# Four moves in one encoder kernel: a split behind a bank's copy, weights in token tiles, stores issued by ScalarE, an earlier load

## The chip, the core and the metric

The kernel runs on one core of a Trainium2 chip. The time is the device time of one execution in microseconds (us). The engines are named as in the profile: PE (TensorE, matmuls; PEld its weight loads), DVE (VectorE), ACT (ScalarE), POOL (GpSimd) and SP (SyncE, which issues nearly all transfers).

## The reference, cut to what matters

One encoder layer with two groups of heads over the same normalised input, for two sequences with the same weights: the prompt (512 tokens) and the sample (1024 tokens).

```python
def mixer_layer(x, norm_g, w_in, w_dw, b_dw, ln_g, ln_b, w_pw, sink, w_out):
    h = rms_norm(x, norm_g)
    z = h @ w_in                      # 2048 -> 3*1024 + 2*1024 + 2*256
    c_val, c_glu, c_gate, q, k, v, a_gate = split(z)
    q, k = apply_rope(q), apply_rope(k)
    conv_out = conformer_conv(c_val, c_glu, w_dw, b_dw, ln_g, ln_b, w_pw) * silu(c_gate)
    attn_out = banded_sink_attention(q, k, v, sink) * silu(a_gate)   # window 128, sinks
    return x + concatenate([conv_out, attn_out]) @ w_out
# encoder: the layer, then rms_norm, for x_prompt and for x_sample; all in float32
```

## The kernel before, in words

**Matmuls in three passes.** Float32 operands are split into a high part and a low rest (`parts`, L499 and L500: ScalarE copies the high part, VectorE subtracts it to get the low one), and each product of 128x128 weights with 128x512 tokens is three matmuls: high with high, high with low, low with high.

**Units.** The sample's projections run as units of seven products in place of eight (a Strassen scheme). A `Unit` covers 8 weight tiles of 128x128 in each of two column blocks. It has two raw loads (`load0`, `load1`) and four weight operands made from them (`make0` to `make3`). The products run in the order P1, P2, P6, P5, P7, P3, P4, 12 matmuls each; P1 and P2 use the first operand, P6 and P5 the second, P7 and P3 the third, P4 the fourth. P1 writes bank a, P2 bank b, P6 adds onto bank a, P5 writes bank c, P7 adds onto bank a, P3 onto c, P4 onto a. When a product is done, `tap` takes its bank up: for all but P2 and P3 ScalarE copies the bank (L226), and VectorE adds. P6 can start only when P1's bank a has been copied. The third operand is a subtraction on VectorE (L142), the split's high part on ScalarE (L499) and the low part on VectorE (L500). Most items of the program are one unit ("lone"); a few are two side by side. `Onto` is a unit that adds its products onto tiles on VectorE (L293) without a copy by ScalarE.

**Jobs.** The prompt's projections and others are plain jobs (`Job`, 48 matmuls each, L652) with two weight loads. Some read the low part back from memory, where the units had stored it, and ScalarE then makes the high part alone (L407).

**Order and rings.** `run` goes through the items; around the matmuls it calls `w_prep`, which makes operands ahead of their use (`look` of them) and issues the next loads, and `tick`, which lets three lanes of other work (convolution, attention, sums) move on at given rates. The instructions are put into each engine's queue by priority: `URGENT` work is placed early, `issue_after` keeps an instruction behind another. An engine runs its queue in order, so an instruction that waits holds all behind it. Tiles come from rings: 3 raw weight buffers, 3 split operands, 4 each of "a", "g", "u" and "p", 7 of "f". A load into a ring's tile waits until the former tile there is no longer read.

**The places.** The sample's last gates: `silu_of` makes the gate's Silu on ScalarE and stores it (`store` issues on SP, L493). The last unit before the prompt's jobs (`end`) also splits the prompt's tokens (`follow`, `load_two`, from xr_d, mostly in "a" tiles). `prompt.jobs()` follow: `pj[0]` is the prompt's first job, with the attention of the sample beside it. Late in the jobs `attention_sums` runs (L1266, L1267), and after it the prompt's attention group by group: `group` loads keys and values (k_d, v_d) into "a" tiles and the query (q_d) into a "u" tile.

Of the kernel before, what the change touches and what calls it, by code (L numbers as in the profile page):

```python
# [7 lines left out]
F32 = mybir.dt.float32  # L8
# [85 lines left out]
class Unit:  # L94
# [34 lines left out]
    late = False  # L129
    look = NHL  # L130
# [31 lines left out]
    def make2(self):  # L162
        self.sub(self.r2[:, 0], self.r2[:, 1], self.r2[:, 0])
        if self.sums:
            self.e.store(self.sums["P7"], self.r2[:, 0])
        t = self.e.hl_tile()
# [19 lines left out]
    def product(self, step, late):  # L186
# [11 lines left out]
        for j in range(HALF):  # L198
# [21 lines left out]
    def tap(self, name):  # L220
# [3 lines left out]
        if name not in ("P2", "P3"):  # L224
            t = e.E()
            nc.scalar.activation(t, bank, AF.Copy)  # L226
        if name == "P1":
# [147 lines left out]
class Job:  # L375


    behind = False
# [7 lines left out]
    def preps(self, e):  # L386
        def one(k):
# [3 lines left out]
            def load():  # L391
                st["raw"] = e.raw_tile()
# [27 lines left out]
class Encoder:  # L420
# [203 lines left out]
    def run(self, items):  # L624
# [3 lines left out]
        for n, item in enumerate(items):  # L628
# [3 lines left out]
            if isinstance(item[0], Unit):  # L632
                for u in item:
                    u.open()
# [93 lines left out]
class Sequence:  # L728


    def __init__(self, e, s):
# [3 lines left out]
        self.hT = {}  # L735
        nc = e.nc
# [358 lines left out]
    def group(self, g):  # L1095
# [7 lines left out]
        held = []  # L1103
        for src in (self.k_d[g], self.v_d[g]):
            held.append(e.A([self.T], F32))
            nc.sync.dma_start(held[-1], src)
        self.load_query(g, 0)
# [7 lines left out]
    def load_query(self, g, b):  # L1115
        if b < self.B:
            self.q = self.e.U([GROUP, P])
# [66 lines left out]
    def units(self):  # L1184
# [16 lines left out]
        for i in range(0, NC, 2):  # L1201
            done = each(self.silu_of(self.gate_d[i]), self.silu_of(self.gate_d[i + 1]))
# [29 lines left out]
class Mix:  # L1232
# [590 lines left out]
def encoder(ctx, tc, a):  # L1823
# [161 lines left out]
    pj[0].behind = True  # L1985
# [13 lines left out]
    def prepare():  # L1999
# [4 lines left out]
        e.attn.add(mix.attention_sums())  # L2004
# [120 lines left out]
```

## Time and profile before

| | us |
|---|---|
| three runs | 2091.29, 2093.96, 2093.98 (median 2093.96) |
| the profiled execution | 2092.61 |
| its span, first to last instruction | 2090.8 |
| PE, DVE, ACT, POOL busy | 2063.2, 1753.9, 1046.4, 77.4 |

The mean clock granted to TensorE was 0.997 of full speed. In the rows of the trace stand the start and the duration in us, the engine and its line, what is written and read with the shape, how many such instructions stand together (x12), and in brackets how long the engine stood idle before and what ended that wait. A matmul's end is modelled, and matmuls overlap; so starts are the safer numbers.

### The profile page before, as it was taken

How to read it: one execution, taken by the hardware profiler on the slowest of the kernel's cores; microseconds unless marked ns; L12 is line 12 of the kernel's file. 1: busy time of each engine (PE TensorE's matmuls, PEld its weight loads, DVE VectorE, ACT ScalarE, POOL GpSimd, SP SyncE). 2: the span in 40 equal slices, each digit the busy share in tenths (PEclk: the TensorE clock that was granted, in tenths of full speed). 3: DMA queues.
4: the chain of work that ended last, by engine and by line, in shares of the span. 5: the costliest groups of instructions: out<-in, count | busy, mean ns of one | idle time of the engine just before them, and what ended most of it. 6: DMA issues, size and time to landing. Idle time of an engine off the chain costs nothing.

```text
span 2090.8 us, 27085 instructions
## 1 busy us (share of the span) xinstructions
PE 2063.2 (99%) x9259; PEld 1695.2 (81%) x9259; DVE 1753.9 (84%) x2877; ACT 1046.4 (50%) x1711; POOL 77.4 (4%) x92
## 2 busy tenths in 40 slices
PE   9999999999999999999999999999999999999998
PEld 8878888888887778778888888887888878888886
DVE  8758899998899999999556877776899978898887
ACT  7476435333464344544456777336454343454454
POOL 0001110000001112100000000000000000000000
PEclk9999999999999999999999999999999999999999
DMA  8988887865577676945455565996789889678897
GB/s 279 320 294 244 204 214 234 292 201 170 181 240 194 169 170 179 273 153 161 162 170 185 168 193 166 324 334 222 242 291 300 282 291 318 211 246 297 290 332 269
DMA packets 251194, 494.54 MB, mean 237 GB/s; under 512 B 23600, under 2 KB 84400, under 8 KB 251056
## 3 DMA queue, kind: packets, MB, share of 16 engines
q1 hardware_dynamic: 238384, 469.75, 67.0%
q0 software_dynamic: 12672, 23.07, 6.6%
q8 instruction: 72, 1.18, 0.2%
q14 instruction: 66, 0.54, 0.1%
HBM read 331.77 MB, written 160.96 MB: 236 GB/s over the span
## 4 chain that ended last, share of the span: by engine, by line
PE 51%; DVE 8%; DMA 4%; issue 3%; ACT 1%; SPq 0%; POOL 0%; ACTq 0%; DVEq 0%; POOLq 0%
PE a L652 13%; PE c L652 7%; PE b L652 6%; PE a L200 6%; PE c L200 3%; PE pv L1166 2%; PE s L1137 2%; PE a L1800 2%; PE s L1800 2%; DVE hl L500 1%; PE b L200 1%; PE pt L1171 1%; PE pv L1800 1%; PE pt L1800 1%; DVE f L1020 1%
## 5 line engine op out<-in xcount | busy, mean ns | idle before, releaser
L200 PE MATMUL a<-t,hl 128*128 128x512 f32 x2640 | 634.0, 391 | 7.8 <-ACT g L226 3.6
L200 PEld LDWEIGHTS a<-t,hl 128*128 128x128 f32 x2640 | 492.8, 188 | 117.2 <-ACT u L226 6.0
L499 ACT ACTIVATE hl<-raw 128x1024 fp32r<-128x1024 f32 (+3 forms) x334 | 297.2, 890 | 394.1 <-PE c L200 85.6
L500 DVE TENSOR_TENSOR hl<-raw,hl 128x1024 fp32r<-128x1024 f32 (+3 forms) x334 | 338.5, 1014 | 134.0 <-ACT hl L499 132.8
L652 PE MATMUL a<-t,hl 128*128 128x512 f32 x1344 | 329.3, 395 | 2.0 <-ACT hl L499 1.4
L200 PE MATMUL c<-t,hl 128*128 128x512 f32 x1320 | 319.9, 390 | 0.6 <-DVE u L293 0.6
L652 PEld LDWEIGHTS a<-t,hl 128*128 128x128 f32 x1344 | 249.4, 189 | 53.0 <-ACT hl L499 1.9
L200 PEld LDWEIGHTS c<-t,hl 128*128 128x128 f32 x1320 | 247.2, 188 | 52.6 <-DVE u L293 1.5
L1020 DVE SCALAR_TENSOR_TENSOR f<-f,c_w_dw,f 128x512 f32<-128x512 f32 x248 | 175.3, 748 | 0.3
L652 PE MATMUL c<-t,hl 128*128 128x512 f32 x672 | 165.4, 394 | 0.0
L652 PE MATMUL b<-t,hl 128*128 128x512 f32 x672 | 163.5, 392 | 0.2 <-DVE hl L500 0.2
L983 DVE SCALAR_TENSOR_TENSOR f<-f,c_w_dw,f 128x512 f32<-128x512 f32 x232 | 163.3, 745 | 0.2 <-ACT f L978 0.2
L200 PE MATMUL b<-t,hl 128*128 128x512 f32 x660 | 160.1, 389 | 0.0
L652 PEld LDWEIGHTS b<-t,hl 128*128 128x128 f32 x672 | 124.9, 188 | 25.3 <-DVE hl L500 0.7
L652 PEld LDWEIGHTS c<-t,hl 128*128 128x128 f32 x672 | 125.3, 189 | 24.7
L200 PEld LDWEIGHTS b<-t,hl 128*128 128x128 f32 x660 | 123.7, 188 | 25.5
L1012 DVE SCALAR_TENSOR_TENSOR f<-f,w_both,f 128x512 f32<-128x512 f32 x120 | 89.9, 749 | 1.8
L407 ACT ACTIVATE hl<-raw 128x1024 fp32r<-128x1024 f32 x44 | 46.5, 1057 | 61.6 <-PE a L652 22.6
L226 ACT ACTIVATE u<-a 128x512 f32<-128x512 f32 x82 | 48.6, 592 | 56.1 <-PE a L200 50.8
L226 ACT ACTIVATE g<-a 128x512 f32<-128x512 f32 x78 | 46.2, 593 | 56.7 <-PE a L200 54.4
L499 ACT ACTIVATE a<-pt 128x512 fp32r<-128x512 f32 x64 | 38.0, 594 | 68.3 <-PE pt L1171 68.2
L1151 ACT ACTIVATE p<-p,tiny 128x384 f32<-128x384 f32 (+1 forms) x96 | 54.5, 570 | 33.0 <-DVE tiny L1148 22.5
(332 smaller groups left out, 2637.7 us busy)
## 6 DMA issues: line engine op xcount, KB each, us to landing
raw<-w_in SPq DMA_DIRECT2D x171, 512.0 KB, 5.0
raw<-w_out SPq DMA_DIRECT2D x31, 512.0 KB, 5.0
raw<-w_pw SPq DMA_DIRECT2D x24, 512.0 KB, 4.2
wsum_P<-raw SPq DMA_DIRECT2D x47, 256.0 KB, 3.5
raw<-wsum_P SPq DMA_DIRECT2D x18, 512.0 KB, 4.6
f<-x_s SPq DMA_DIRECT2D x16, 512.0 KB, 7.2
g<-wsum_P SPq DMA_DIRECT2D x28, 256.0 KB, 4.4
a<-sum_S SPq DMA_DIRECT2D x24, 256.0 KB, 5.8
```

The lines of the kernel that those rows point to most:

```text
L200: nc.tensor.matmul(acc, hl[:, l, o, j, :], toks[j][:, r], start=name in FRESH and j == 0 and q == 0, stop=name in LAST and j == HALF - 1 a ...
L226: nc.scalar.activation(t, bank, AF.Copy)
L407: e.nc.scalar.activation(t[:, 0], raw, AF.Copy)
L499: nc.scalar.activation(hi, x, AF.Copy)
L500: nc.vector.tensor_tensor(lo, x, hi.bitcast(F32), ALU.subtract)
L652: nc.tensor.matmul(job.acc[0], hl[:, l, kk // HALF, kk % HALF, :], r, start=i == 0 and p == 0, stop=i == nk - 1 and p == 2,)
L983: nc.vector.scalar_tensor_tensor(t, h[:, j : j + T], w(j), t, ALU.mult, ALU.add)
L1012: nc.vector.scalar_tensor_tensor(m0, odd[:, j : j + H], both(j), m0, ALU.mult, ALU.add)
L1020: nc.vector.scalar_tensor_tensor(out, d[:, j : j + H], w(2 * j + k), out if j else m0, ALU.mult, ALU.add)
L1137: nc.tensor.matmul(ps[:, 0:n], qs[:, x, h], k[y][:, keys], start=p == 0, stop=p == 2)
L1151: nc.scalar.activation(p[:, 0:n], p[:, 0:n], AF.Exp, bias=nm[:, h : h + 1], accum_out=l[:, h : h + 1])
L1800: nc.tensor.matmul(acc[t], self.toks[name, m][:, x, i, t * P : (t + 1) * P], parts[i][l].rearrange("p a b -> p (a b)"), start=fresh and fi ...
```

## The change

Four edits.

1. The third operand's subtraction is separated (`less2`). In a lone unit VectorE does it during P1 (`lessen`), where before the whole third operand was prepared. The split follows in step 1, during P2, and is kept behind the last copy of a bank by ScalarE (`issue_after(self.copied)`). For `Onto` units there is no such copy and only the step changes.
2. The prompt's first job loads both its weight tiles into "a" tiles and not into the raw ring (`early`).
3. The sample's gates 4 to 7 (of 8) are stored by ScalarE's own queue: eight transfers.
4. The prompt's first keys, values and query are loaded into "p" tiles just before the last step of `attention_sums` (`fetch_first`), not after it into "a" and "u" tiles.

```diff
+    def less2(self):
+        self.sub(self.r2[:, 0], self.r2[:, 1], self.r2[:, 0])
+        if self.sums:
+            self.e.store(self.sums["P7"], self.r2[:, 0])
+        self.lessened = True
+
     def make2(self):
-        self.sub(self.r2[:, 0], self.r2[:, 1], self.r2[:, 0])
-        if self.sums:
-            self.e.store(self.sums["P7"], self.r2[:, 0])
+        if not self.lessened:
+            self.less2()
         t = self.e.hl_tile()
-        self.e.parts(t[:, 0], t[:, 1], self.r2)
+        with self.e.tc.issue_after(self.copied) if self.copied else ExitStack():
+            self.e.parts(t[:, 0], t[:, 1], self.r2)
...
-                e.w_prep(i + self.look)
+                if step or not self.alone:
+                    e.w_prep(i + self.look)
+                else:
+                    e.lessen(self)
...
             nc.scalar.activation(t, bank, AF.Copy)
+            self.copied = nc.cur_bb.bb.instructions[-1]
...
-                st["raw"] = e.raw_tile()
+                st["raw"] = e.A([2, HALF, P], F32) if self.early else e.raw_tile()
...
+    def lessen(self, unit):
+        if self.ready == unit.at[2]:
+            with ExitStack() if self.calm else self.tc.high_priority(URGENT):
+                unit.less2()
...
-    def silu_of(self, dst):
+    def silu_of(self, dst, own=False):
+        queue = self.e.nc.scalar if own else self.e.nc.sync
...
-            self.e.store(dst[:, t * W : t * W + W], z)
+            queue.dma_start(dst[:, t * W : t * W + W], z)
...
-            done = each(self.silu_of(self.gate_d[i]), self.silu_of(self.gate_d[i + 1]))
+            done = each(*(self.silu_of(self.gate_d[j], i >= 4) for j in (i, i + 1)))
...
+    def fetch_first(self):
+        self.held[0] = self.fetch(0, lambda: self.e.PT("p", NP, [W]))
+        self.load_query(0, 0, self.e.PT("p", NP, [GROUP, P]))
...
-    def attention_sums(self):
+    def attention_sums(self, then):
...
         for j in range(HALF):
+            if j == HALF - 1:
+                then()
...
-    pj[0].behind = True
+    pj[0].behind = pj[0].early = True
...
-        e.attn.add(mix.attention_sums())
+        e.attn.add(mix.attention_sums(prompt.fetch_first))
```

Three places show what moves. Lines below 126 keep their numbers or shift by one; L226, L493 and L499 of before are L236, L504 and L510 of the changed kernel. ScalarE in the last unit but one before the prompt's jobs; `hl_908` of before and `hl_910` of the changed kernel are the third operand, `g_911` and `g_909` P1's copy. Before:

```order
L226 ACTIVATE u_907_7216<-a_889_7061 128x512
L499 ACTIVATE hl_904_7195<-p_903_7191 128x512
L499 ACTIVATE hl_908_7220<-raw_892_7072 128x1024
L226 ACTIVATE g_911_7239<-a_906_7212 128x512
L499 ACTIVATE hl_912_7257<-raw_888_7049 128x512
```

and in the changed kernel:

```order
L236 ACTIVATE u_907_7216<-a_889_7061 128x512
L510 ACTIVATE hl_904_7195<-p_903_7191 128x512
L236 ACTIVATE g_909_7234<-a_906_7212 128x512
L510 ACTIVATE hl_910_7236<-raw_894_7088 128x1024
L510 ACTIVATE hl_912_7257<-raw_888_7049 128x512
```

The third operand's split and the copy have changed places.

SP's queue where the prompt's first job is fed; `raw_945` and `a_945` are the second half of job 0's weights, `raw_959` and `raw_964` the two halves of job 1's, `xr_d` the prompt's tokens, `k_d0`, `v_d0` and `q_d0` the sample's keys, values and query. Before:

```order
L393 DMA raw_945_7447<-w_in 128x1024
L399 DMA hl_946_7449<-low_kv0_0_361 128x1024
L1963 DMA a_937_7407<-xr_d1_7_193 128x1024
L493 DMA gate_d0_5_93<-g_918_7318 128x512
L493 DMA gate_d0_5_93<-u_914_7277 128x512
L1106 DMA a_970_7589<-k_d0_0_104 128x1024
L1106 DMA a_971_7591<-v_d0_0_106 128x1024
L393 DMA raw_959_7515<-w_in 128x1024
L493 DMA gate_d0_4_92<-u_931_7380 128x512
L1118 DMA u_972_7593<-q_d0_0_108 128x4x128
L493 DMA gate_d0_6_94<-g_939_7413 128x512
L393 DMA raw_964_7581<-w_in 128x1024
```

In the changed kernel, where `raw_959` stands further ahead, in the row that was job 0's first half's:

```order
L1995 DMA a_925_7366<-xr_d1_3_189 128x1024
L410 DMA hl_946_7449<-low_kv0_0_361 128x1024
L404 DMA raw_964_7581<-w_in 128x1024
L1995 DMA a_936_7406<-xr_d1_6_192 128x1024
L1995 DMA a_937_7408<-xr_d1_7_193 128x1024
L404 DMA a_945_7447<-w_in 128x1024
L404 DMA raw_976_7633<-w_in 128x1024
L1148 DMA u_972_7593<-q_d0_0_108 128x4x128
L412 DMA hl_965_7583<-low_kv0_1_362 128x512
L1138 DMA a_970_7589<-k_d0_0_104 128x1024
L1138 DMA a_971_7591<-v_d0_0_106 128x1024
```

The gates' stores are gone, the weights of job 1 come ahead of job 0's second half, the query ahead of keys and values, and a token tile (`a_925`) is loaded here that was loaded further ahead before.

ScalarE at the same place in the changed kernel; `gate_d` rows are the stores it now issues:

```order
L510 ACTIVATE hl_961_7552<-a_921_7347 128x1024
L982 ACTIVATE g_939_7414<-g_939_7414 128x512
L982 ACTIVATE u_931_7380<-u_931_7380 128x512
L983 DMA gate_d0_6_94<-g_939_7414 128x512
L983 DMA gate_d0_4_92<-u_931_7380 128x512
L418 ACTIVATE hl_946_7449<-a_945_7447 128x1024
L236 ACTIVATE g_973_7596<-a_930_7376 128x512
L418 ACTIVATE hl_965_7583<-raw_964_7581 128x1024
L510 ACTIVATE a_984_7698<-u_972_7593 128x512
L514 ACTIVATE t1_955_7501<-a_937_7408,c_norm_g_278 128x512
L514 ACTIVATE t1_956_7504<-a_937_7408,c_norm_g_278 128x512
L510 ACTIVATE hl_975_7630<-raw_959_7515 128x1024
```

The query's split (`a_984`) stands ahead of the prompt's last tokens (`t1_955`, `t1_956`) and of job 1's first operand (`hl_975`); two stores stand between the operands of job 0.

More of the change, by code (lines that the diff above doesn't have):

```diff
@@ L129 @@
     late = False
+    alone = lessened = copied = False
     look = NHL
@@ L160, in make1 @@
         return t
-    def make2(self):
+    def less2(self):
         self.sub(self.r2[:, 0], self.r2[:, 1], self.r2[:, 0])
@@ L165, in make2 @@
             self.e.store(self.sums["P7"], self.r2[:, 0])
+        self.lessened = True
+    def make2(self):
+        if not self.lessened:
+            self.less2()
         t = self.e.hl_tile()
-        self.e.parts(t[:, 0], t[:, 1], self.r2)
+        with self.e.tc.issue_after(self.copied) if self.copied else ExitStack():
+            self.e.parts(t[:, 0], t[:, 1], self.r2)
         self.r2 = None
@@ L375 @@
 class Job:
-    behind = False
+    behind = early = False
     def __init__(self, w, ks, n, rhs, evac, before=None, low=None):
@@ L633, in run @@
                 for u in item:
+                    u.alone = len(item) == 1
                     u.open()
@@ L735, in __init__ @@
         self.hT = {}
+        self.held = {}
         nc = e.nc
@@ L1102, in group @@
             k, v = [(t[:, 0], t[:, 1]) for t in kv]
[L1103 to L1107, printed above, removed]
+        held = self.held.pop(g, None)
+        if not held:
+            held = self.fetch(g, lambda: e.A([self.T], F32))
+            self.load_query(g, 0)
         yield e.attn.rate * LEAD * (1 + (self.s and g == 0))
```

10 lines of the change are left out of this document (8 added, 2 removed).

## The prediction

> **What bounds the kernel now.** I read the profile's page first, then the waits of TensorE, then the timeline of TensorE around each wait, and beside it that of the engine that ended it.
>
> The page's line of busy times:
>
> ```profile
> PE 2063.2 (99%) x9259; PEld 1695.2 (81%) x9259; DVE 1753.9 (84%) x2877; ACT 1046.4 (50%) x1711; POOL 77.4 (4%) x92
> L200 PE MATMUL b<-t,hl 128*128 128x512 f32 x660 | 160.1, 389 | 0.0
> ```
>
> TensorE (PE) is busy for 99% of the span of 2090.8 us and the change takes no matmul away, so all that can be gained are the places where it stands still or runs slowly. The second line counts the units: 12 matmuls fall on bank b in each, 660 / 12 = 55 units of seven products. The view of TensorE's waits names what it stood still for (total, times, longest):
>
> ```profile
> PE a L200 <- ACT g L226: 3.6, 4, 1.4
> PE s L1137 <- DVE tiny L1140: 2.5, 1, 2.5
> PE a L200 <- ACT u L226: 2.4, 5, 0.8
> PE s L1137 <- ACT a L499: 1.6, 1, 1.6
> PE a L652 <- ACT hl L499: 1.4, 1, 1.4
> PE s L724 <- DVE u L719: 1.2, 1, 1.2
> PE a L200 <- DVE u L293: 1.0, 2, 0.8
> ```
>
> Together 13.7 us, so this change deals in microseconds and not in per cents. 0.2% of the time (4.2 us) is about what a measurement of this kernel can tell from no change.
>
> **Part 1, the third operand's split.** TensorE, ScalarE (ACT) and VectorE (DVE) in one lone unit, by the timeline (start, duration; idle before in brackets):
>
> ```profile
> 669.59 2.91 PE L200 MATMUL b<-t,hl 128*128 128x512 f32 x12
> 673.80 3.03 PE L200 MATMUL a<-t,hl 128*128 128x512 f32 x12 [1.30 <-ACT g L226]
> 676.67 2.88 PE L200 MATMUL c<-t,hl 128*128 128x512 f32 x12
> 679.39 0.85 PE L200 MATMUL a<-t,hl 128*128 128x512 f32 x3
> 671.44 0.68 DVE L142 TENSOR_TENSOR raw<-raw 128x512 f32<-128x512 f32 x1
> 672.21 1.06 ACT L499 ACTIVATE hl<-raw 128x1024 fp32r<-128x1024 f32 x1 [4.68 <-issue]
> 673.17 0.58 ACT L226 ACTIVATE g<-a 128x512 f32<-128x512 f32 x1
> ```
>
> P2 (bank b) starts at 669.59, so P1 on bank a was issued by then, and its copy (L226) could have run some 2 us before P6 wants the bank. It ran only at 673.17, because the split of the third operand (L499) stands ahead of it and waits for VectorE's subtraction, which ended at 672.12. A product takes 679.39 − 676.67 = 2.72 us; from P2's start to P6's it took 4.21. The stall so costs 1.49 us, 0.2 more than the idle time shown.
>
> In the changed program the copy stands ahead of the split. The copy then needs only the bank, and 2.72 us of P2 cover its 0.58 us and an activation of 1.06 us that may still be running: the stall goes to nothing. The split comes 0.6 us later on ScalarE, and its operand is wanted at P7 only, four products or 10.9 us after the unit's start, so that is covered too. The waits from 600 to 850 us:
>
> ```profile
> PE a L200 <- ACT g L226: 2.3, 3, 1.3
> PE a L200 <- ACT u L226: 1.1, 3, 0.4
> ```
>
> Six stalls, 3.4 us idle, and with 0.17 us of restart each **4.4 us**; all six are of P2-to-P6 kind. The same edit takes the split out of three other places:
>
> ```profile
> 150.97 0.50 PE L724 MATMUL s<-u,ones_r 128*128 128x512 f32 x1 [1.20 <-DVE u L719]
> 149.31 1.22 DVE L500 TENSOR_TENSOR hl<-raw,hl 128x1024 fp32r<-128x1024 f32 x1
> 166.09 4.19 PE L200 MATMUL a<-t,hl 128*128 128x512 f32 x17 [0.82 <-ACT u L226]
> 163.44 1.28 ACT L499 ACTIVATE t<-p 128x512 fp32r<-128x512 f32 x2 [2.03 <-DMA p<-sum_S]
> 1809.61 2.99 PE L200 MATMUL a<-t,hl 128*128 128x512 f32 x12 [0.79 <-DVE u L293]
> 1807.03 1.23 DVE L500 TENSOR_TENSOR hl<-raw,hl 128x1024 fp32r<-128x1024 f32 x1
> 1808.77 0.69 DVE L293 TENSOR_TENSOR u<-a,u 128x512 f32<-128x512 f32 x1
> ```
>
> At 150.97 TensorE waits for four small VectorE operations between which the split's low half (1.22 us) was put; it now stands behind them: 1.20 + 0.17, say **1.4 us**. At 166.09 the copy stood behind splits that waited 2.03 us for a load; it now stands ahead of the later ones: 0.82 + 0.17 = **1.0 us**, or nothing if an earlier split waits as long. At 1809.61 the sum into bank a's tile (L293) stood behind the same 1.22 us; the two are swapped: **0.9 us**. Against this I set two new waits of about 1 us each, for rows that changed place nowhere else shown: an estimate from the mean of the stalls quoted here, **−2 us**, bounds 0 and −5.
>
> **Parts 2 and 3, the first job.** TensorE from the last unit into the prompt's job 0 and job 1:
>
> ```profile
> 862.12 3.04 PE L200 MATMUL a<-t,hl 128*128 128x512 f32 x12 [0.44 <-ACT u L226]
> 865.85 10.72 PE L652 MATMUL b<-t,hl 128*128 128x512 f32 x46 [0.24 <-DVE hl L500]
> 878.01 0.73 PE L652 MATMUL a<-t,hl 128*128 128x512 f32 x2 [1.44 <-ACT hl L499]
> 879.26 5.97 PE L652 MATMUL a<-t,hl 128*128 128x512 f32 x25 [0.53 <-DVE hl L500]
> 890.98 1.02 PE L1137 MATMUL s<-t,a 128*128 128x256 f32 x6 [2.48 <-DVE tiny L1140]
> 891.85 3.97 PE L652 MATMUL a<-t,hl 128*128 128x512 f32 x10
> 874.91 1.06 ACT L407 ACTIVATE hl<-raw 128x1024 fp32r<-128x1024 f32 x1 [8.80 <-DMA raw<-w_in]
> 865.65 0.33 SPq L393 DMA_DIRECT2D raw<-w_in  x1
> 834.79 0.33 SPq L393 DMA_DIRECT2D raw<-w_in  x1
> ```
>
> The idle times are 0.44 + 0.24 + 1.44 + 0.53 + 2.48 = 5.1 us, with the restarts 6.0. Behind the longest the ten matmuls of 891.85 take 3.97 us where 227 ns each (2.72 / 12) would be 2.3: 1.7 us at half the clock. Together 7.7 us. The 1.44 us gap did not halve the clock, the 2.48 us gap did. By the Trainium skill (TensorE: Matmul & The Clock Gate, section "Why this matters for your kernels") gaps over about 3 us are to be avoided for that reason; here 2.48 us were enough, so the trace sets the bound lower, and by the page alone the 1.7 us would not be there to win.
>
> The cause is in the last rows: the weights of job 1's second half were issued at 865.65 and read at 874.91, 9.3 us later, and ScalarE sat 8.80 us with the split of job 1's first half queued behind, which TensorE waits for at 878.01. Now both loads of job 0 go to tiles outside the ring, and job 1's first half takes the place in SP's queue that job 0's first half had, 834.79; its second half comes behind it, near 852. So the 1.44 and 0.53 us go, and the 0.24 at job 0's start. What comes instead:
>
> - The early tile takes one that held the prompt's tokens. Their load (a, from xr_d) now waits until another of these tiles has been split, and is issued about where the tokens after it were:
>
> ```profile
> 850.09 0.32 SPq L1963 DMA_DIRECT2D a<-xr_d  x1
> raw<-w_in SPq DMA_DIRECT2D x171, 512.0 KB, 5.0
> 853.36 2.88 PE L200 MATMUL c<-t,hl 128*128 128x512 f32 x12
> ```
>
>   With a little under the 5.0 us of the weights' loads, which are as large, it lands near 854.6. ScalarE has then, by the order of its rows, stood at the tokens' two splits with nothing else to do from about 852.6; behind them wait a third split, a Silu and the copy of P6's bank, which P7 wants when the product of 853.36 ends, at 856.1. At some 0.6 us each the copy ends near 857.8: a new stall of **1.7 us**, bounds 0 (a landing in 3 us) and 4.
> - The eight stores on ScalarE's queue. The nearest row is SP's issue of such a store, 0.32 us; ScalarE is busy 50%, so 8 × 0.32 = 2.6 us lie in its idle time. A store waits for its Silu, which stands just ahead on the same engine, and for the landing of an older transfer on its semaphore; that can hold what follows it. On SP nothing waits any more for these Silus, and the keys' and query's loads stand otherwise.
> - The query's load waits until a store has landed, and its split stands ahead of the prompt's last tokens and of job 1's weights. I put the scores' stall (2.48 before) at 1.4, with a second of 0.8, and the clock not halved: 2.2 us with restarts, bounds 0 and 4.3 (as before).
>
> So 7.7 becomes 1.7 + 2.2, **3.8 us gained**, bounds −0.6 and +7.7.
>
> A rule of the Trainium skill speaks against part 3 (DMA: Bandwidth & Descriptors, section "Issuing engines are not separate DMA queues"): transfers of all engines run on the same 16 DMA engines, and another issuing engine saves only issue time. The 9.3 us above agree that the transfer, not its issue of 0.33, is the long part. It is a rival below.
>
> **Part 4, the prompt's keys.**
>
> ```profile
> 1421.59 0.74 PE L1137 MATMUL s<-f,a 128*128 128x256 f32 x4 [1.57 <-ACT a L499]
> 1420.91 0.63 ACT L499 ACTIVATE a<-u 128x512 fp32r<-128x512 f32 x1 [0.85 <-DMA u<-q_d]
> 1414.92 1.25 SPq L1118 DMA_DIRECT2D u<-q_d  x2
> ```
>
> The scores wait for the query's split, and that for a load issued 6 us before. Now keys, values and query are issued some 20 us earlier into the p ring. But then the scores too are due earlier, by some 60 matmuls, near 1406, and the split needs an a-tile that the attention sums' last multiply frees; that waits for a load which now stands behind others on SP. I find the split ready at about 1407.6: a stall of 1.6 in place of 1.57. **0**, bounds −2 and +2; cover gone costs the 2, no halved clock.
>
> **The sum.** 4.4 + 1.4 + 1.0 + 0.9 − 2.0 + 3.8 + 0 = 9.5 us. The profiled execution took 2092.6 us (span 2090.8, 1.8 around it), the median of the runs is 2094.0 and they spread from 2091.3 to 2094.0. 2092.6 − 9.5 = **2083.1 us**. The bounds, all the gains full and no new wait, give 2092.6 − 4.4 − 3.3 − 7.7 − 2 = 2075; the other ends of parts 2 to 4 with −5 for part 1's new waits give 2092.6 − 7.7 + 5 + 1 + 2 = 2093.
>
> **Rivals.**
>
> 1. *The first job stays as slow.* By the rule above the loads land as late as before, because the same 16 engines carry them, and the stores' new queue frees nothing. For it: the 9.3 us from issue to use. Against: job 1's loads have another place in SP's queue, ahead of what they stood behind. Only part 1 is left: 2092.6 − 7.7 + 2 = 2086.9. Chance 0.15.
> 2. *ScalarE is held by its own stores or the query's split.* If the query takes the 9.3 us of the weights' load after a store that took the same, it lands near 878; the prompt's last tokens behind it, wanted at 875.6, and job 1's weights come some 4 us late, the clock halves (1.7), and the later scores stall as before. That is about 6 us more than before in this section: 2092.6 − 7.7 + 2 + 6 = 2092.9, no change. It decides when the query lands after about 874. Chance 0.12.
> 3. *The weights ring slips, and the kernel is slower.* The third split frees a raw buffer, and the next load into it is issued after it. The split comes up to 1.5 us later in every lone unit (672.21 to behind the copy, 0.6 us, plus what else VectorE takes first). If the loads have no slack for this, operands are late in each unit: at 0.3 us in each of 55 units 16.5 us, so 2092.6 − 9.5 + 16.5 = 2099.6. For it: the raws take 5.0 us at the median and 9.3 under load. Against: no wait of TensorE between 600 and 850 us is for a load, and the longest for a split's low half is 0.4. It decides when the slack is under some 1 us. Chance 0.11.
> 4. *All of it works and nothing new waits*: 2075 as above. Chance 0.05.
>
> **How the numbers follow.** The forecast has 0.57, its own range 2079 to 2088. The time is its 2083.1. The range for 8 in 10 takes in rival 1 and part of rival 2 and leaves out 3 and the end of 4: 2078 to 2092. Faster by over 4.2 us (below 2089.8): the forecast (0.56 of it), rivals 1 (0.14) and 4 (0.05), 0.75 together. Within 0.2%: rival 2 and the ends of the others, 0.13. Slower: rival 3 and its neighbours, 0.12.
>
> **What would show it.** Right: in the changed profile the copies (L236 there) of P1 in lone units end before P2 does, and the wait of a L207 for ACT falls from 6.0 us to under 4, left over mostly at 143 us (behind a load of x_s) and near 856. No TensorE wait for hl at the start of job 1, no stretch of 427 ns matmuls near 890. The scores near 1406 still wait 1 to 2 us. Wrong: any unit's P7 waiting for its operand, ScalarE's stores followed by idle times of over 2 us near 860 to 878, or hl waits for raw loads that recur in many units.

## The result, and the profile after

| | before | changed |
|---|---|---|
| median of 18 runs each | 2093.97 us | 2089.23 us |
| profiled execution (span) | 2092.61 (2090.8) | 2089.18 (2087.4) |
| last matmul starts at | 2081.2 | 2076.4 |

The ratio is 0.9984, 95% interval 0.9977 to 0.9991: 3.4 us faster (1.9 to 4.8). The medians of the table lie 4.7 us apart; the ratio, since it has an interval, is used from here on. The sign and the range of the forecast held; its size did not, 3.4 us where 9.5 were summed up.

The page's busy times and ScalarE's new queue in the changed kernel:

```profile
PE 2061.6 (99%) x9259; PEld 1696.7 (81%) x9259; DVE 1753.4 (84%) x2877; ACT 1042.1 (50%) x1711; POOL 77.2 (4%) x92
q10 hardware_dynamic: 1152, 2.10, 0.3%
```

TensorE's waits there (total us, times, longest):

```profile
PE a L207 <- ACT u L236: 5.7, 4, 3.6
PE a L207 <- ACT g L236: 2.6, 4, 1.1
...
PE s L741 <- DVE u L736: 1.2, 1, 1.2
```

ScalarE's stores (queue q10) take 0.3% of the time of the 16 DMA engines. The waits for job 1's operands (1.4), for the first job's scores (2.5) and for the prompt's query (1.6) are gone. But the waits for ScalarE's copies, 6.0 us before, are 8.3 now, with one of 3.6; the prediction had set under 4 as a sign of being right. Between 600 and 846 us the same view shows that edit 1 did what it was to do there:

```profile
PE s L207 <- DVE hl L511: 0.5, 1, 0.5
PE a L207 <- ACT g L236: 0.4, 2, 0.2
PE a L207 <- ACT u L236: 0.2, 1, 0.2
```

The longest wait now stands in the last unit before the prompt's jobs. TensorE, ScalarE and SP by the timeline:

```profile
848.91 3.03 PE L207 MATMUL a<-t,hl 128*128 128x512 f32 x12 [1.10 <-ACT g L236]
851.78 2.88 PE L207 MATMUL c<-t,hl 128*128 128x512 f32 x12
858.24 4.61 PE L207 MATMUL a<-t,hl 128*128 128x512 f32 x12 [3.58 <-ACT u L236]
862.68 2.90 PE L207 MATMUL c<-t,hl 128*128 128x512 f32 x12
868.15 11.04 PE L669 MATMUL b<-t,hl 128*128 128x512 f32 x48
879.03 6.29 PE L669 MATMUL a<-t,hl 128*128 128x512 f32 x27
...
855.24 1.33 ACT L514 ACTIVATE t<-a,c_norm_g 128x512 fp32r<-128x512 f32 x2 [3.59 <-DMA a<-xr_d]
857.61 0.57 ACT L236 ACTIVATE u<-a 128x512 f32<-128x512 f32 x1
...
849.24 0.32 SPq L1995 DMA_DIRECT2D a<-xr_d  x1
```

In the last unit P6 starts at 848.91, P5 at 851.78, P7 at 858.24. P7 was due at 851.78 + 2.72 = 854.50 and started 3.74 us later. Its twelve matmuls then took 862.68 − 858.24 = 4.44 us in place of 2.72, 1.7 us at half the clock. The wait is the one forecast, with the load, the splits and the copy in the order forecast, but it costs 5.4 us and not 1.7. Job 0 (868.15, 879.03) runs without a gap. At P6 (848.91) there is a wait of 1.1 us that the kernel before did not have.

Two new kinds of wait elsewhere, in the same timeline: first the one at 351 us, then a small one that comes three times, at 639, 775 and 834 us:

```profile
351.55 1.65 PE L207 MATMUL a<-t,hl 128*128 128x512 f32 x6 [1.53 <-ACT u L236]
349.86 1.06 ACT L898 ACTIVATE f<-f 128x1024 f32<-128x1024 f32 x1 [1.09 <-DMA f<-x_p]
350.91 0.58 ACT L236 ACTIVATE u<-a 128x512 f32<-128x512 f32 x1
...
775.46 1.88 PE L207 MATMUL a<-t,hl 128*128 128x512 f32 x7 [0.25 <-ACT g L236]
773.57 0.69 DVE L974 TENSOR_TENSOR g<-g,f 128x512 f32<-128x512 f32 x1
774.29 0.63 ACT L982 ACTIVATE g<-g 128x512 f32<-128x512 f32 x1 [2.39 <-DVE g L974]
```

At 351 the copy of P6's bank, which P7 wants, has come to stand behind a square (L898) that waits for a load of x_p. At 775 the low half of the third operand's split, now done during P5, holds up the gate's multiply (L974), this the Silu (L982), and the Silu the copy of the bank.

Last, the end of the program gave a little back. Before:

```profile
2070.56 11.04 PE L1759 MATMUL a<-t,t 128*128 128x512 f32 x48
2081.64 0.69 DVE L1694 TENSOR_TENSOR f<-a,f 128x512 f32<-128x512 f32 x1 [0.78 <-PE a L1759]
```

and in the changed kernel:

```profile
2065.75 11.04 PE L1791 MATMUL a<-t,t 128*128 128x512 f32 x48
2078.05 0.68 DVE L1726 TENSOR_TENSOR f<-a,f 128x512 f32<-128x512 f32 x1
```

TensorE's last job starts 4.8 us earlier; VectorE's sum behind it, which had waited for TensorE, starts 3.6 us earlier and now follows other work of VectorE. So 4.8 us on TensorE became 3.4 in the span.

### The profile page after: what moved, and what is told of

Same layout as the page of the kernel before. It is cut to its first block, busy times and chain, and to the rows that moved or that the text cites. A ratio compares the mean times of both kernels' runs of the same rounds, so it can differ in the third digit from the quotient of the medians.

```text
span 2087.4 us, 27041 instructions
## 1 busy us (share of the span) xinstructions
PE 2061.6 (99%) x9259; PEld 1696.7 (81%) x9259; DVE 1753.4 (84%) x2877; ACT 1042.1 (50%) x1711; POOL 77.2 (4%) x92
## 4 chain that ended last, share of the span: by engine, by line
PE 49%; DVE 7%; issue 6%; DMA 4%; POOL 1%; ACT 1%; SPq 0%; ACTq 0%; POOLq 0%; DVEq 0%
PE a L669 14%; PE b L669 7%; PE c L669 6%; PE a L207 6%; PE c L207 3%; PE pv L1196 2%; PE s L1167 2%; PE a L1832 2%; DVE hl L511 2%; PE b L207 1%; PE pt L1201 1%; PE s L1832 1%; DMA p<-y_d 1%; DVE t L511 1%; DMA u<-part_out 1%
## 5 line engine op out<-in xcount | busy, mean ns | idle before, releaser
L510 ACT ACTIVATE hl<-raw 128x1024 fp32r<-128x1024 f32 (+3 forms) x333 | 295.1, 889 | 385.3 <-PE c L207 86.0
L1040 DVE SCALAR_TENSOR_TENSOR f<-f,c_w_dw,f 128x512 f32<-128x512 f32 x248 | 174.0, 746 | 0.3
L236 ACT ACTIVATE u<-a 128x512 f32<-128x512 f32 x82 | 48.5, 592 | 70.5 <-PE a L207 68.6
L236 ACT ACTIVATE g<-a 128x512 f32<-128x512 f32 x78 | 46.3, 593 | 67.9 <-PE a L207 65.9
L510 ACT ACTIVATE a<-pt 128x512 fp32r<-128x512 f32 x64 | 37.9, 593 | 67.1 <-PE pt L1201 66.8
L511 DVE TENSOR_TENSOR a<-pt,a 128x512 fp32r<-128x512 f32 x64 | 44.0, 687 | 27.5 <-ACT a L510 26.6
```

What stands on the lines that cost most here:

```text
L510: nc.scalar.activation(hi, x, AF.Copy)
L511: nc.vector.tensor_tensor(lo, x, hi.bitcast(F32), ALU.subtract)
L1040: nc.vector.scalar_tensor_tensor(out, d[:, j : j + H], w(2 * j + k), out if j else m0, ALU.mult, ALU.add)
```

## The experiments

A profile is one execution, and two executions of one kernel differ by microseconds. So TensorE's lost time was worked out for the profiled execution of every kernel from the starts of its matmuls: the distance between two, less the usual one for the shape (227 ns for 128x512), summed over stretches between the same matmuls, named by the times of the kernel before. This is "the loss" below; waits, restarts and half clock (matmuls at about twice the usual distance) are all in it. Each series of runs was made on one chip, beside runs of the kernel before there, to which its ratios refer; a kernel has 5 to 12 runs in them.

The first question was whether the terms of the sum were wrong one by one, or each held and their gains were waited for again further on.

**One edit at a time.** Against the kernel before. Edit 1 alone is the pieces of the diff with `less2`, `copied` and `lessen`. Edit 2 alone:

```diff
-                st["raw"] = e.raw_tile()
+                st["raw"] = e.A([2, HALF, P], F32) if self.early else e.raw_tile()
...
-    pj[0].behind = True
+    pj[0].behind = pj[0].early = True
```

Edit 3 alone:

```diff
-            self.e.store(dst[:, t * W : t * W + W], z)
+            queue.dma_start(dst[:, t * W : t * W + W], z)
...
```

Edit 4 alone, with `fetch_first` as above:

```diff
...
+            if j == HALF - 1:
+                then()
...
```

> Before with edit 1 alone (third operand's split behind the copy). Theory A (the copy's waits only move in part): the six P2-to-P6 stalls of 600 to 850 us (4.4 us) are gone, four P5-to-P7 stalls of 0.3 to 0.4 us (1.4) stand in their place, a P7 stall of about 1.7 us near 351, the prompt's first job as before (stalls 1.4 and 2.5, half clock for some 8 matmuls). Sum of TensorE's losses about 2 us less than before. Rival B (the new stalls in the changed kernel come from the other edits): losses 6 us less, no P5-to-P7 stall over 0.3.

> Before with edit 2 alone (both weight tiles of the prompt's job 0 in token tiles). Theory A (the displaced token tile is what costs): a P7 stall of 2 to 4 us near 856 to 860 behind the token tile's load, with the half clock after it if the stall is over 2.5; no stall at job 1's start and no 2.5 us stall of the scores, so about 0 to -2 us in all. Rival B (the stores on SP are what held job 1's weights): the stall at job 1's start of 1.4 us and that of the scores stay, and the token stall comes on top: 2 to 5 us slower.

> Before with edit 3 alone (eight gate stores on ScalarE's queue). Theory A: the raw ring still holds job 1's weights back; stalls at job 1's start and of the scores as before, 0 plus or minus 1 us. Rival B: with the stores off SP job 1's weights come in time: stalls of 1.4, 0.5 and 2.5 us and the half clock gone, 5 to 6 us faster.

> Before with edit 4 alone (prompt's first keys, values and query in p tiles before the last step of the attention sums). Theory A: the scores' stall of 1.6 us at 1421 goes and nothing takes its place: 2 us faster. Rival B (as predicted): the scores come some 60 matmuls earlier and wait about as long for the query's split: 0, and the changed kernel's gain there came from the other edits' shift.

Measured: edit 1 1.0002 (0.9991 to 1.0014), edit 2 0.9990 (0.9980 to 1.0001), edit 3 1.0010 (0.9999 to 1.0021), edit 4 0.9990 (0.9979 to 1.0000). Edit 1 gains nothing by itself, although its stalls between 640 and 760 us are gone (loss there 0.8, before 4.8). Edit 2 takes the loss of the last unit and the first jobs from 8.8 to 4.4 us. Edit 3 leaves that loss at 9.9: the waits for job 1's operands and for the scores stay (2.06 and 2.27 us, before 1.44 and 2.48). Edit 4 removes the scores' stall (loss from 1380 to 1430 us 0.4, before 2.3).

**All but one, and half of edit 2.** Against the changed kernel: edit 2 undone, edit 3 undone, edit 1 undone; and only the second half of job 0's weights in a token tile:

```diff
-                st["raw"] = e.A([2, HALF, P], F32) if self.early else e.raw_tile()
+                st["raw"] = e.A([2, HALF, P], F32) if self.early and k else e.raw_tile()
```

> The changed kernel without edit 2 (job 0's weights in the raw ring again; edits 1, 3, 4 stay). Theory A: no P7 stall at the token tile (the 3.7 us and the half clock after it are gone), but job 1's weights are late again, with stalls of 1.4 and 2 us or more after 878: about as fast as the changed kernel, within 2 us. Rival B (the stores' queue feeds job 1): neither stall, 5 us or more faster than the changed kernel.

> The changed kernel with only the second weight tile of job 0 in a token tile; the first stays in the raw ring, so all early token tiles load as before the change. Theory A: the token stall of 3.7 us and the half clock of 1.7 us are gone and job 1's weights still come in time: 4 to 6 us faster than the changed kernel. Rival B: job 1's second half, now a row later on SP, is late, a stall of 1 to 2 us at 878 and the scores' stall come back: 1 to 3 us faster than the changed kernel.

> The changed kernel without edit 3 (edits 1, 2, 4). Theory A (edit 3 costs): the gates' stores are on SP again, 2 to 4 us faster than the changed kernel. Rival B (edit 3 helps only beside edit 1, and edit 1 costs without it): 1 us or more slower than the changed kernel, and slower than edits 2 and 4 alone by 3 us or more.

> The changed kernel without edit 1 (edits 2, 3, 4 stay). Theory A (edit 1 is worth nothing net, since its new stalls of 1.4 at P7, 1.3 in the last unit and 1.3 near 351 take back the 4.4): P2-to-P6 stalls of 4.4 us are back, those three kinds are gone, the token stall shrinks by about the 1 to 2 us that TensorE comes later: as fast as the changed kernel, within 2 us. Rival B (edit 1 is the gain, as predicted): 4 us or more slower than the changed kernel, no faster than before.

Measured: without edit 2 0.9988 (0.9975 to 1.0000), with half of it 0.9984 (0.9974 to 0.9994), without edit 3 0.9986 (0.9977 to 0.9994), without edit 1 1.0013 (1.0004 to 1.0022). Without edit 2, and with half of it, the token tile comes in time and job 0 waits instead. TensorE without edit 2, then with half of it:

```profile
869.36 10.76 PE L669 MATMUL b<-t,hl 128*128 128x512 f32 x46 [2.85 <-DVE hl L511]
```

```profile
868.25 12.26 PE L669 MATMUL b<-t,hl 128*128 128x512 f32 x46 [2.62 <-DVE hl L511]
```

Without edit 1 another wait came up, which makes that kernel slow (loss of the section 8.6). TensorE in job 0, ScalarE and SP there:

```profile
873.15 8.11 PE L652 MATMUL b<-t,hl 128*128 128x512 f32 x22 [2.79 <-ACT hl L407]
872.04 1.06 ACT L407 ACTIVATE hl<-a 128x1024 fp32r<-128x1024 f32 x1 [7.63 <-DMA a<-w_in]
863.71 0.63 SPq L1131 DMA_DIRECT2D u<-q_d  x1
864.45 0.55 SPq L393 DMA_DIRECT2D a<-w_in  x1
```

and the view of SP's waits from 840 to 870 us:

```profile
SPq L1131 <- DMA gate_d<-u: 6.2, 1, 6.2
```

SP's queue waits 6.2 us for the landing of a gate that ScalarE stored, before it may issue the query's load; job 0's second weights stand behind that load in this order, and TensorE waits 2.79 us for their split. This is akin to rival 2, in that the query waits for a store; but what is held is SP's queue with the weights, not ScalarE by the query's split. In the changed kernel the same wait is 4.4 us, but the weights stand ahead of the query and it costs nothing.

**Edits 2 and 4 alone, and the changed kernel again.** Against the changed kernel, edits 1 and 3 undone (the main lines below), in two series of runs; and the changed kernel itself once more, beside the second of them.

```diff
-        with self.e.tc.issue_after(self.copied) if self.copied else ExitStack():
-            self.e.parts(t[:, 0], t[:, 1], self.r2)
+        self.e.parts(t[:, 0], t[:, 1], self.r2)
...
-            queue.dma_start(dst[:, t * W : t * W + W], z)
+            self.e.store(dst[:, t * W : t * W + W], z)
```

> Before with edits 2 and 4 alone. Theory A (the gain is that of these two): the sum of their single gains, some 4 us faster than before, as fast as the changed kernel or faster. Rival B (they gain only with the copies in the new order): 0 to 2 us faster than before.

> Edits 2 and 4 alone once more, beside the changed kernel on the same chip. Theory A: 1 to 3 us faster than the changed kernel there. Rival B: equal within 1 us, the earlier difference being that of the chips.

> The changed kernel as it is, for comparison on the same chip: 3 to 5 us faster than before. Its TensorE stalls at the token tile (3.7 us and half a clock), at P7 (1.4), near 351 (1.7) and in the last unit (1.3) should be there again if they belong to the program's order and not to one execution.

Measured: the pair 0.9975 (0.9966 to 0.9983) and 0.9977 (0.9968 to 0.9986), the changed kernel 0.9983 (0.9974 to 0.9993). Two edits do at least as much as all four; the difference of 1.5 us is inside the intervals. TensorE at the token tile with the pair:

```profile
855.56 2.88 PE L200 MATMUL c<-t,hl 128*128 128x512 f32 x12
859.37 3.01 PE L200 MATMUL a<-t,hl 128*128 128x512 f32 x12 [0.93 <-ACT u L226]
```

859.37 − 855.56 − 2.72 = 1.09 us, in the first of its two series; no wait at P6 before it, and no half clock behind it. With edit 1 beside it (the changed kernel, its repeat and the kernel without edit 3) P6 stands idle 1.1 to 1.4 us and P7 2.4 to 3.6. The loss of the section is 4.4, 4.2 and 6.2 us in the three kernels with edit 2 and without edits 1 and 3, and 7.4, 7.3 and 7.8 in those three with edit 1.

**Moving the wait.** Against the changed kernel: token tiles 6 to 9 loaded into "p" tiles and the later ones afterwards; the same with the last unit as before; and edits 2 and 4 with edit 1 in the lone units of 640 to 850 us alone, the last excepted.

```diff
-        if 8 <= j < 12:
+        if 6 <= j < 10:
...
-                    u.alone = len(item) == 1
+                    u.alone = len(item) == 1 and u.look == NHL
...
+                    u.alone = u.some
+    for u in stages[3][2:-1]:
+        u.some = True
```

> The changed kernel with the token tiles shared out differently: tokens 6 to 9 in the p ring, 10 and 11 in a token tile that is loaded after the first split, 12 to 15 as then come free; no token tile has to wait for another that is wanted in the next two products. Theory A (the displaced tile costs 3.7 us and a half clock of 1.7): both gone, job 1 still fed in time: 4 to 5 us faster than the changed kernel. Rival B (the wait is passed on): the load of tokens 10 and 11 or 14 and 15 holds ScalarE instead and the first job's weights or P3 wait 2 us or more: within 2 us of the changed kernel.

> As the kernel with shared-out token tiles, and with edit 1 left out in the last unit before the prompt's jobs. Theory A: the stall of 1.3 us at that unit's P6 (copy behind three token splits) is gone as well, 1 us faster than with the token tiles alone. Rival B: that stall comes from the token splits' own place and stays.

> Edits 2 and 4, and edit 1 only in the lone units of 640 to 850 us without the last of them. Theory A (edit 1 is good only where the copy waited): the P2-to-P6 stalls of 4.4 us go, P5-to-P7 stalls of about 1.2 come, nothing changes near 351 and in the Onto units; TensorE reaches the prompt's tokens 3 us earlier than with edits 2 and 4 alone and waits there up to that much longer: 0 to 3 us faster than edits 2 and 4 alone. Rival B: the order of the queues at the first job turns again, and the section loses 3 us or more: slower than edits 2 and 4 alone.

Measured: 0.9991 (0.9982 to 1.0000), 0.9988 (0.9979 to 0.9998) and 0.9974 (0.9963 to 0.9985). With the tokens moved their stall goes, and the weights come behind the query as in the kernel without edit 1:

```profile
875.83 4.58 PE L669 MATMUL b<-t,hl 128*128 128x512 f32 x12 [2.35 <-ACT hl L418]
866.34 0.67 SPq L404 DMA_DIRECT2D a<-w_in  x1
```

With the last unit as before, P6 there still waits 1.1 us. And with edit 1 upstream alone, the last unit untouched, P6 and P7 in it wait 1.05 and 3.33 us. So the two waits do not come from what edit 1 does in the last unit; they come from what it does ahead of it. (In both kernels the order of ScalarE's rows in that unit is still the changed kernel's, with three token splits ahead of the copy that P6 wants and the third operand's split behind it; in the kernel before two stand ahead, and the split too.) The wait was not removed by giving the tokens other tiles, only passed on.

**Who takes the gain back.** The windows view gives the busy time of each engine in stretches (start:end, length; PE, PEld, DVE, ACT, POOL, then clock, DMA share and GB/s). The kernel before, one row, then the changed kernel:

```profile
640.00:700.00 60.00, 58.29 (x262) 47.00 (x261) 59.62 (x90) 23.37 (x37) 10.55 (x12) 1.00 0.70 178
...
640.00:700.00 60.00, 60.00 (x273) 49.61 (x272) 59.65 (x90) 25.07 (x40) 10.62 (x13) 1.00 0.69 173
838.00:855.00 17.00, 15.56 (x68) 12.21 (x66) 16.97 (x27) 7.44 (x12) 3.49 (x4) 1.00 0.89 241
```

VectorE, 84% busy on the whole, is 99% busy in these stretches; from 640 to 855 us it is busy for 210 of 215 us, and for 209 in the kernel before. It was full before the change too. Two rows of the changed kernel show how TensorE comes to wait for it at P6 of the last unit. ScalarE's split of a "p" tile waits for VectorE's subtraction into it (L143), and behind that split stand a Silu, a copy, three token splits and the copy that P6 wants:

```profile
844.13 0.68 DVE L143 TENSOR_TENSOR p<-raw,raw 128x512 f32<-128x512 f32 x1
844.85 0.63 ACT L510 ACTIVATE hl<-p 128x512 fp32r<-128x512 f32 x1 [1.15 <-DVE p L143]
```

This subtraction starts 0.8 us ahead of P2 (844.93) in the changed kernel. In the nine kernels with edit 1 in the units ahead and this filler it starts 0.5 to 0.8 us ahead of P2, and P6 waits in each; in the seven without edit 1 it starts 2.9 to 3.0 us ahead (there L142), and P6 waits in none. What SP waits for before it issues the token tile's load is VectorE too (SP's waits, 846 to 850 us):

```profile
SPq L1995 <- DVE t L515: 2.2, 1, 2.2
```

Much of VectorE's work there is filler: the sample's convolution, let in at 0.3 of the matmuls' time. Four kernels change that one number. In three of them, the changed kernel, the pair, and the changed kernel without edit 3, there is less filler in this stretch. Its work then comes behind 855 us; none is left out. Between the same matmuls of 600 to 855 us the changed kernel has 54 of VectorE's filler multiplies (L1040), and 46 with less filler, 4.9 us less; the number of ScalarE's instructions there stays the same:

```diff
-RATES = (0.4, 0.6, 0.3, 1.0, 0.5)
+RATES = (0.4, 0.6, 0.27, 1.0, 0.5)
```

and the pair with more of it:

```diff
-RATES = (0.4, 0.6, 0.3, 1.0, 0.5)
+RATES = (0.4, 0.6, 0.33, 1.0, 0.5)
```

> The changed kernel with the convolution's filler paced at 0.27 and not 0.3 of the matmuls' time in the sample's last projections (600 to 855 us): some 7 us of VectorE's work there move behind 855 us; nothing is left out. Theory (VectorE, busy 97 to 99% from 640 to 855 us, sets the pace, so what the third operand's later split gains TensorE there is waited for in the last unit): the last unit's stalls fall from 1.1 at P6 and 2.6 to 3.6 at P7 to under 0.4 and under 2, without half clock; TensorE's loss from the last unit to job 1 falls from 7.3-7.4 to 4 to 5.5 us; ratio to before 0.9965 to 0.9975. Rival (the token tile's load lands 5 to 6 us after its issue and decides, whatever VectorE does): P7 still waits 2.5 us or more, loss 7 to 8, ratio 0.998 to 0.9985.

> Edits 2 and 4 alone with the same slower filler (0.27). Theory (VectorE sets the pace from 640 to 855 us): without the later split too VectorE is what TensorE waits for there, so TensorE's loss from 600 to 840 us falls from 7.7-7.8 to 5 to 7 and the last unit's P7 stall from 0.9-1.2 to under 0.6; ratio 0.9965 to 0.9975. Rival (the load decides): loss within 1 us of 7.7, P7 stall 0.8 to 1.5, ratio 0.9975.

> Edits 2 and 4 alone with a faster filler (0.33): some 7 us more of VectorE's work between 600 and 855 us. Theory (VectorE sets the pace): the last unit now waits although the third operand's split is where it was: a stall of over 0.8 at P6 and over 2.2 at P7, TensorE's loss from the last unit to job 1 up from 4.2-6.2 to over 7; ratio 0.9985 to 1.0005. Rival (the load decides): P7 0.8 to 1.5 as before this edit, loss under 6.2, ratio 0.997 to 0.998.

> Edits 1, 2 and 4 (the gates' stores stay on SP) with the slower filler (0.27); a try at a version that beats both. Theory (VectorE sets the pace): as in the changed kernel with the slower filler, loss from the last unit to job 1 down from 7.8 to 4 to 5.5, ratio 0.9965 to 0.9978. Rival (the load decides): loss 7 to 8, ratio 0.9986 as without the slower filler.

| kernel | ratio to before | loss 640–760 us | loss 760–838 | loss last unit and first jobs |
|---|---|---|---|---|
| before | 1 | 4.8 | 1.5 | 8.8 |
| changed | 0.9984 | 0.3 | 1.7 | 7.4 |
| changed, less filler | 0.9963 (0.9950 to 0.9976) | 0.1 | −0.2 | 4.2 |
| changed without edit 3, less filler | 0.9963 (0.9949 to 0.9977) | 0.1 | −0.2 | 4.5 |
| edits 2 and 4 (two series) | 0.9975, 0.9977 | 4.5, 5.0 | 1.6, 1.6 | 4.2, 6.2 |
| edits 2 and 4, less filler | 0.9965 (0.9953 to 0.9977) | 2.2 | −0.2 | 3.7 |
| edits 2 and 4, more filler | 1.0006 (0.9995 to 1.0017) | 5.9 | 1.8 | 7.6 |

TensorE in the last unit: the changed kernel with less filler (P6, P5, P7), and the same without edit 3 (P6, P5, P7):

```profile
853.98 2.88 PE L207 MATMUL a<-t,hl 128*128 128x512 f32 x12
856.70 2.88 PE L207 MATMUL c<-t,hl 128*128 128x512 f32 x12
861.46 4.26 PE L207 MATMUL a<-t,hl 128*128 128x512 f32 x12 [1.88 <-ACT u L236]
```

```profile
854.52 2.88 PE L207 MATMUL a<-t,hl 128*128 128x512 f32 x12
857.25 2.88 PE L207 MATMUL c<-t,hl 128*128 128x512 f32 x12
860.37 3.06 PE L207 MATMUL a<-t,hl 128*128 128x512 f32 x12 [0.24 <-ACT u L236]
```

and the pair with more filler (P6, and P4, the last product):

```profile
855.38 3.04 PE L200 MATMUL a<-t,hl 128*128 128x512 f32 x12 [1.48 <-ACT g L226]
867.98 3.01 PE L200 MATMUL a<-t,hl 128*128 128x512 f32 x12 [1.41 <-ACT u L226]
```

With less work on VectorE the wait at P6 is gone in both kernels that have edit 1. P7 waits 861.46 − 856.70 − 2.72 = 2.04 us in the one (with half clock still, against the expectation) and 0.40 in the other; the last product of the second waits 0.9. With more work the wait at P6 comes without edit 1. The expected size at P7 was wrong there: P7 does not wait, P4 does.

For P6 this settles the cause. The subtraction of L143 starts 4.6 and 5.5 us ahead of P2 in the two kernels with edit 1 and less filler, 5.0 in the pair with less filler, and 0.7 in the pair with more: of these four P6 waits in the last alone. VectorE's pace sets how early TensorE can pass this point.

For P7 VectorE is only a part. From the changed kernel to the one with less filler the token tile's load is issued 0.4 us earlier against P5, is used 5.3 us after its issue in place of 6.0, and a third token split has moved behind the copy, 0.6 us; without edit 3 the earlier issue is 1.4 of 2.1 us. In the pair with other filler, more or less, the copy that P7 wants no longer stands behind the late token tiles, so P7 there says nothing about the load. How long the load takes is thus a cause of its own for P7; no run changes that time alone.

Both kernels of 0.9963 are faster than the kernel before, by 7.8 us where the change alone gave 3.4 (intervals 0.9950 to 0.9976 and 0.9977 to 0.9991). The changed kernel did not run beside them, they have 6 and 8 runs, and the interval of its repeat (0.9974 to 0.9993) touches theirs; that they beat it is likely, not shown. With less filler the pair without edit 1 is as fast as the full change with it (0.9965, of 5 runs, and 0.9963). So about half of the stalls that edit 1 removes are stalls of a full VectorE too: with less filler the pair's loss between 600 and 838 us falls from 7.8 and 7.7 to 3.7 without edit 1.

## Why the prediction was right or wrong

Most of what it named happened. What failed is that its terms were added as if each gain would reach the end. Part 1 was to give 5.7 us with its new waits counted, and 2.7 at its lowest bound; edit 1 alone measured 1.0002 (0.9991 to 1.0014).

- **Part 1, the six stalls (4.4).** Right in their place: from 640 to 760 us the eight kernels with edit 1 in the lone units (one of them not in the last) and the old filler lose 0.4 us on the mean, the seven without it 4.4. The step that failed is behind it: "a stall goes" was not followed by asking what is late next. VectorE was full there, so TensorE only ran up to it: +0.5 from 760 to 838 us, and from the last unit to the first jobs, with edit 2, +2.6 (7.5 against 4.9).
- **The other three places (3.3).** From 130 to 170 us the changed kernel loses 3.0 in place of 4.4, the wait at 166 gone; on the mean it is 3.5 with edit 1 and 3.7 without, next to nothing. At 150 the split went and VectorE finished 1.3 us earlier, but the order put TensorE's matmul earlier by about as much, and it still waits 1.2 (L741 among the waits). Around 1809 the wait went, and others came: 3.9 us of loss from 1700 us on before and after.
- **The two new waits (−2).** A guess without a place. One is the copy behind the square at 351 us: 1.0 to 1.8 us in the eight kernels with edit 1, 0.1 on the mean without. It was to be seen in the order of ScalarE's rows at that place.
- **Parts 2 and 3, the first job (3.8).** Without edit 1 the size was right: the loss of the section falls from 8.6 (three kernels without edits 1 and 2) to 4.9, 3.7 us, and the token tile's stall of 1.7 is measured as 1.1 to 1.4. In part that is luck: the scores' stall, put at 2.2, is gone there, and job 0's start, put at no wait, stands idle 1.2 to 1.6 us. With edit 1 it falls from 8.8 to 7.5 only, 1.3 us. The term that was mis-sized is the token tile's stall, 1.7 forecast and 3.7 + 1.7 of half clock measured. Its load was issued at 849.24 and used at 855.24, 6.0 us later in place of 4.5, and TensorE came 1.6 us earlier than taken (854.5, not 856.1). The eight stores' issues took 0.33 to 0.35 us each, near the 0.32 estimated.
- **Part 4 (0).** Not more than about 1 us. In the changed kernel the stall is gone, since the query's split was ready at 1401.2 and not at 1407.6; in the kernel without edit 3 it waits. The scores, then ScalarE's split, in the changed kernel; and the scores without edit 3:

```profile
1402.05 1.20 PE L1167 MATMUL s<-f,a 128*128 128x256 f32 x6
1400.56 0.63 ACT L510 ACTIVATE a<-p 128x512 fp32r<-128x512 f32 x1 [3.38 <-DVE a L1303]
```

```profile
1406.21 0.51 PE L1165 MATMUL s<-f,a 128*128 128x256 f32 x2 [1.27 <-ACT a L510]
```

  The loss from 1380 to 1430 us is 1.8 to 3.8 in the four kernels without edit 4 and 0.2 to 4.9 with it: the bounds of ±2 were right, the value is not fixed.

Put together from these means, edit 1 gives −3.9 from 640 to 760 us and takes 1.5 at 351, about 1 in the units from 600 to 640 and 760 to 838, 0.7 near 115 and 2.6 from the last unit on: nothing, or some 2 us lost, as the runs of edits 2 and 4 with and without it show. That leaves 3.7 us of edit 2 and at most 1 of edit 4.

Of the rivals, the first (the first job stays as slow, 2086.9) did not come: job 0 and job 1 start without a wait. The rule behind it, in the Trainium skill (DMA: Bandwidth & Descriptors, "Issuing engines are not separate DMA queues"), agrees with edit 3 alone: with another issuing engine and nothing else the waits at job 1 and at the scores stayed (1.0010). The second did not come as it was put, ScalarE held by the query's split; what came near it is SP's wait for a gate's store, which the order of SP's queue kept off the path, and which made the kernel without edit 1 slow (1.0013), where the order differed. The third did not come: no wait of TensorE for a raw load recurs in the units.

Not settled: how much of the 0.7 us near 115 us is edit 1's (0.4 to 3.9 with it, 0.2 to 1.5 without), and why the two kernels with edit 1 and less filler lose 16 us before 600 us in their profiles, where the others lose 7 to 13; their profiled executions lie at the upper end of their own runs.

## What to carry to other kernels

Before a saving is counted, look at the busy time of every engine in that stretch, not on the whole: VectorE was 84% busy over the kernel and 97 to 98% in the stretch where TensorE was to gain, in the profile of before already, so the gain was given back at the next place where TensorE waits for it. A wait that is removed ahead of a full engine is moved; taking work off the full engine (here 10% less filler) gained as much without the edit as with it. And where a load is issued when another engine frees a tile, its stall can grow by what the waiting engine gains: TensorE was 1.6 us earlier at P7 than the prediction took it to be, and the stall 2.0 us longer.

## What the runs showed of the hardware that was not expected

Whether the clock is halved does not follow from the length of the idle time just before alone. It was halved behind idle times of 1.88 us (4.26 us for twelve matmuls, changed kernel with less filler), 2.35 (4.58, tokens moved) and 3.58 (4.61, changed kernel), where 2.9 to 3.1 us are usual for twelve, but not behind 2.85 us (10.76 us for 46 matmuls, without edit 2), nor behind 2.56 in the repeat of the changed kernel:

```profile
861.44 3.04 PE L207 MATMUL a<-t,hl 128*128 128x512 f32 x12 [2.56 <-ACT u L236]
```

In the second series of edits 2 and 4 it was halved although no single wait was long: behind 1.09 and 0.52 us of idle time, two matmuls apart, 46 matmuls took 12.33 us, in the first series, behind 0.64 and 0.53, 10.74. The granted clock from 855 to 890 us agrees: 0.95 in the changed kernel and that second series, 1.00 in the first and in the kernel without edit 2.

The page of the Trainium skill that the prediction named (TensorE: Matmul & The Clock Gate, "Why this matters for your kernels") puts the gaps to avoid at about 3 us; here 1.88 were enough once, and 2.85 were not another time.

Loads took longer in the stage that was fullest of transfers. The view of transfers in the changed kernel, whole and from 840 to 880 us (times, size, median us from issue to landing):

```profile
raw<-w_in SPq DMA_DIRECT2D x169, 512.0 KB, 5.3
...
raw<-w_in SPq DMA_DIRECT2D x4, 512.0 KB, 6.5
a<-xr_d SPq DMA_DIRECT2D x3, 512.0 KB, 7.2
```

The 16 DMA engines were busy for 0.74 of the time over the whole kernel and 0.90 in that stretch. The prediction took the median of the whole kernel for a load of this stretch; the stretch's own was 1 to 2 us longer, and the kernel before had shown it: 6.3 us for its six loads of weights there, 5.8 for its two of tokens, where the whole has 5.0. That the transfers beside them are the cause is not shown by a run of its own.
